# First quarter of the output weights split beside the prompt's attention, the others in pieces, in a GLA + MLA decoder step

## The chip, the cores and the metric

One core of one Trainium2 chip runs the whole step in one launch. The metric is the device time of an execution in microseconds, the median over several runs. TensorE (PE, with its weight loads PEld) makes all matrix products; VectorE (DVE), ScalarE (ACT) and GpSimd (POOL) do the rest; SyncE (SP) issues most transfers, GpSimd the gathers of cache pages. Each engine takes its instructions in the order in which they stand.

## What is computed

One decoder layer for a prompt of 1024 tokens and 8 samples of 8 new tokens with 8192 cached ones each, all in fp32. The layer norms its input, projects it, and mixes tokens by two groups of heads side by side: gated linear attention (GLA, a recurrence in chunks) and latent attention (MLA, softmax over latent rows; the samples' rows come from a paged cache). The two outputs, 512 columns each, are joined, projected by w_o (1024 x 1024), gated and added to the input; a gated convolutional FFN follows.

```
def mla_attend(q_lat, q_rope, kv, kr, q_pos, k_pos):
    ...
        s = jnp.einsum('bthl,bsl->bhts', ql, kv) + jnp.einsum('bthr,bsr->bhts', qr, kr)
        s = s.astype(jnp.float32) * scale
        s = jnp.where(k_pos[None, :] <= qp[:, None], s, -jnp.inf)
        p = jax.nn.softmax(s, axis=-1).astype(kv.dtype)
        return jnp.einsum('bhts,bsl->bthl', p, kv)
```

## The kernel before

An fp32 product is made as three fp32r products of a high and a low part (`mm3`, L141 to L143): hi x hi, lo x hi, hi x lo. The high part is a cast on ScalarE, the low part a subtraction, mostly on VectorE (L122). Weights go through `block` (L1384): a raw tile `uraw` of 1 MB is loaded by SyncE (L1388), cast to `uhi` (L1393), and subtracted to `ulo`. There are two raw tiles, so the load of a third block waits until the first is subtracted.

The stages are: the input projections; the samples' queries; then two generators that `interleave` draws step by step; then the output projection (`out_proj`), the FFN up and the FFN down. The first generator is `mla_sample`, 32 blocks of 1024 cached keys. For each block GpSimd gathers the rows L (1 MB) and R (256 KB); TensorE transposes them (`kps`, L1227, two PSUM buffers) and ScalarE copies them to KT and KR (L1229); then come the scores S (L1237, L1239), the maximum `rm`, its spread `mg` and `nm` on VectorE, the exponential `p` on ScalarE, its transpose `pt` on VectorE (L1266), the output O (L1271), its sum `on` (L1276). The second is `main`: the prompt's queries, GLA (its rows go from `o_sb` to the DRAM tile `s_mix`, L788), and `mla_prompt`. This one goes over 4 heads: `keys` (products `sps` of a head's key weights `ukr`, split into `uks`), `scores`, `vals`, `values` (probabilities transposed to `pt`, L1158, cast to `pth`, subtracted to `ptl`, products `olps`), then a norm per head (`ob`, sums `hms`) and a store of 256 rows to `s_mix` (L1178). Queries come by `qlr` (L1103) and `qrr` (L1107), the causal mask by `craw` (L1058).

`interleave` is given a total for each generator and always draws from the one whose drawn share of its total is lowest; the sample's instructions get a priority that is put off by up to 450 places, less and less toward its end. A tile scheduler then sets the order on each engine from priorities, dependences, its own model of durations, and free tiles. A pool that is opened late gets its place from the pools closed before it. `main` ends with opening the weights' pools and the gate's, and `out_weights`, four quarters of w_o (256 columns each) through `block`.

`out_proj` takes row blocks `mx` of 128 rows back from `s_mix` (L1419), transposes them (`tps`, L1426), splits them to `mh` and `ml`, and multiplies them by the four quarters (`y`).

Of the kernel before, what the change touches and what calls it, by code (L numbers as in the profile page):

```python
# [11 lines left out]
F32 = mybir.dt.float32  # L12
# [9 lines left out]
P = 128  # L22
# [84 lines left out]
class Kernel:  # L107
# [935 lines left out]
                next(chain, None)  # L1043


    def mla_prompt(self):
        nc, A = self.nc, self.A
        with ExitStack() as es:
            kp = es.enter_context(self.pool("mk"))
            bp = es.enter_context(self.pool("mb", bufs=1))  # L1050
# [3 lines left out]
            pq = es.enter_context(self.pool("psq", bufs=1, space=PSUM))  # L1054
            kTh, kTl = self.kTh, self.kTl
            causal = kp.tile([P, P], F32R, name="causal")
            craw = kp.tile([P, P], F32, name="craw")
            nc.sync.dma_start(craw, A["c_causal"])  # L1058
            nc.scalar.copy(causal, craw)
            def split2(x, name):  # L1060

                n = x.shape[2]
                t = bp.tile([P, TP], F32R, name=name, tag="pp", bufs=4)[:, 0:4 * n].rearrange("p (j a n) -> p j a n", j=2, a=2)
                nc.scalar.copy(t[:, 0], x)
                self.lo(t[:, 1], x, t[:, 0], nc.vector)
                return t

            def keys(h):

                raw = bp.tile([P, 2, P], F32, name="ukr", tag="ukr")  # L1070
                nc.sync.dma_start(raw, A["w_mla_uk"][0, :, h].rearrange("(a p) n -> p a n", p=P))
                uk = split2(raw, "uks")
                K = [kp.tile([P, TP], F32R, name=x, tag=x) for x in ("Kh", "Kl")]
                for s0 in (0, 512):
                    so = slice(s0, s0 + 512)
                    ps = psS.tile([P, 512], F32, name="sps", tag="S")
                    for a in range(2):
                        self.mm3(ps, uk[:, 0, a], uk[:, 1, a], kTh[:, a, so], kTl[:, a, so], a == 0, a == 1)
                    nc.scalar.copy(K[0][:, so], ps)
                    self.lo(K[1][:, so], ps, K[0][:, so], nc.vector)  # L1080
                    yield 1.3
                self.K = K

            def vals(pr):

                uv = split2(self.uv[:, :, 256 * pr:256 * pr + 256], "uvs")
                V = [mv.tile([P, 8, 256], F32R, name=x, tag=x) for x in ("vh", "vl")]
                for j0 in range(0, 8, 2):
                    ps = psS.tile([P, 512], F32, name="sps", tag="S").rearrange("p (j n) -> p j n", j=2)
                    for j in range(2):  # L1090
                        o = slice((j0 + j) * P, (j0 + j + 1) * P)
                        for a in range(2):
                            self.mm3(ps[:, j], kTh[:, a, o], kTl[:, a, o], uv[:, 0, a], uv[:, 1, a], j == 0 and a == 0, j == 1 and a == 1)
                    x = slice(j0, j0 + 2)
                    nc.scalar.copy(V[0][:, x], ps)
                    self.lo(V[1][:, x], ps, V[0][:, x], nc.vector)
                    yield 1.3
                self.V = V
# [83 lines left out]
            for h in range(4):  # L1182
                yield from keys(h)
                for m in range(4):
                    yield from scores(h, m)
                    if len(self.pend) > 1:
                        yield from values(*self.pend.pop(0))
                    if m == 0 and h % 2 == 0:
                        yield from vals(h // 2)
            while self.pend:  # L1190
                yield from values(*self.pend.pop(0))


    def mla_sample(self, es):
# [186 lines left out]
        self.new = o1, m1, l1  # L1381


    def block(self, src, eng, wp=None):  # L1384

        shape = [P, src.shape[1], src.shape[2]]
        raw = self.wp[0].tile(shape, F32, name="uraw", tag="uraw", bufs=2)
        self.nc.sync.dma_start(raw, src)  # L1388
        if wp is None:
            hi, lo = self.pair(shape)  # L1390
        else:
            hi, lo = (wp.tile(shape, F32R, name=x, tag=x, bufs=2) for x in ("uhi", "ulo"))
        self.nc.scalar.copy(hi, raw)  # L1393
        self.lo(lo, raw, hi, eng)
        return hi, lo

    def pair(self, shape, k=None):
# [5 lines left out]
    def out_weights(self):  # L1403
        nc, A = self.nc, self.A
        wo = A["w_o"][0].rearrange("(a p) n -> p a n", p=P)
        self.wo = [self.block(wo[:, :, 256 * q:256 * q + 256], nc.vector) for q in range(4)]

    def out_proj(self, es, ds):
        nc, A = self.nc, self.A
# [275 lines left out]
    def run(self, stop=None):  # L1685
        nc = self.nc
        with ExitStack() as es:
            dp = es.enter_context(self.pool("scratch", space=DRAM))
            self.s_kv = dp.tile([T, LAT + 2 * RO], F32, name="s_kv")
            self.s_qn = dp.tile([4, P, TP], F32, name="s_qn")  # L1690
            self.s_qr = dp.tile([2, P, TP], F32, name="s_qr")
            self.s_qk = dp.tile([4, P, T], F32, name="s_qk")
            self.s_la = dp.tile([T, 256], F32, name="s_la")
            self.s_v = dp.tile([T, 512], F32, name="s_v")
            self.s_r = dp.tile([T, 512], F32, name="s_r")
            self.s_mix = dp.tile([T, D], F32, name="s_mix")
            self.s_x2 = dp.tile([T, D], F32, name="s_x2")
            self.s_gate = dp.tile([2, 65, D], F32, name="s_gate")
            self.s_g = dp.tile([NCH, P, T], F32, name="s_g")
            self.s_ml = dp.tile([1, 512], F32, name="s_ml")  # L1700
            self.cp = cp = es.enter_context(self.pool("const"))
            self.constants(cp)
            self.ada_start(cp)
            fs = es.enter_context(ExitStack())
            gs = es.enter_context(ExitStack())
            ds = es.enter_context(ExitStack())
            with ExitStack() as zs, ExitStack() as xs:
                self.zp = zs.enter_context(self.pool("z"))
                self.xp = xs.enter_context(self.pool("x", bufs=2, side="right"))
                self.phase1()  # L1710
                if stop == "z":
                    return
                with ExitStack() as es2:
                    self.sample_queries(zs, xs, ds, es2)
                    if stop == "q":
                        return

                    mk = es2.enter_context(self.pool("mkT", side="right"))

                    def main():  # L1720
                        yield from self.prompt_queries(self.prompt_keys(mk, self.nq, self.pq))
                        zs.close()
                        yield from self.gla()
                        yield from self.mla_prompt()
                        self.wp = [fs.enter_context(self.pool(f"fw{j}")) for j in range(2)]
                        self.gt = gs.enter_context(self.pool("gate"))
                        self.out_weights()
                        yield 0.0

                    self.ep = es2.enter_context(self.pool("me", bufs=1, side="right"))  # L1730
                    self.interleave((self.mla_sample(es2), 429.0, 450), (main(), 244.5, 0))
            if stop == "mix":
                return
            with ExitStack() as hs:
                with self.pool("pt", bufs=2, space=PSUM) as self.pt, self.pool("pu", space=PSUM) as self.pu:
                    hT = self.out_proj(hs, ds)
                    gs.close()
                    if stop == "wo":
                        return
                    self.ffn_up(hT)  # L1740
                    if stop == "up":
                        return
            self.ffn_down()
# [35 lines left out]
```

## Time and profile before

| | us |
|---|---|
| median of 3 runs | 1860.03 |
| lowest, highest | 1857.51, 1861.93 |
| profiled execution, its own time | 1861.26 |
| span in its trace | 1859.5 |
| TensorE busy | 1797.6 |
| VectorE busy | 930.1 |
| ScalarE busy | 708.9 |
| GpSimd busy | 529.8 |

The span is what the trace covers, from the first to the last instruction; the execution's own time has 1.8 us around it. A row of the trace's timeline gives start, duration, engine, line, operation, the tiles written and read, and shapes; in brackets is the idle time of the engine before it and what ended that. PE rows of a few products that follow each other are put into one. SyncE's rows (SPq) show the time that the issuing took, waits within it included.

### The profile page before, as it was taken

What the parts mean: (1) busy time and instruction counts of PE and PEld (TensorE: products, weight loads), DVE (VectorE), ACT (ScalarE), POOL (GpSimd) and SP (SyncE); (2) the same over time, 40 slices, a digit from 0 to 9 for tenths busy, and PEclk for the clock granted to TensorE, in tenths of its full rate; (3) what the DMA queues carried; (4) which work ended last, traced back from release to release, by engine and by line L of the source; (5) the groups of instructions that cost most, each with busy time, mean ns of one, the idle gap of its engine ahead of it and who ended that gap; (6) DMA issues with size and microseconds to landing.
All of it is one profiled execution on the core that took longest, in us unless ns stands there. A gap on an engine that the chain in (4) does not pass through costs nothing.

```text
span 1859.5 us, 30758 instructions
## 1 busy us (share of the span) xinstructions
PE 1797.6 (97%) x12403; PEld 1500.4 (81%) x12403; DVE 930.1 (50%) x1680; ACT 708.9 (38%) x1398; POOL 529.8 (28%) x567
## 2 busy tenths in 40 slices
PE   6999999999999999999799999999999999999998
PEld 3888766765665776777499999999999999788787
DVE  3731233347784555565556755554545554523433
ACT  2461111455666666667523422222222222323322
POOL 2640100423554223323011133333333331202221
PEclk7999999999999999999899999999999999999999
DMA  8255552666655555455542412111222111834463
GB/s 300 87 160 181 181 172 75 248 210 199 212 197 166 203 196 173 161 184 181 181 149 104 137 65 71 65 59 65 72 70 70 65 61 61 266 98 136 146 183 96
DMA packets 170618, 265.26 MB, mean 143 GB/s; under 512 B 18278, under 2 KB 118694, under 8 KB 162283
## 3 DMA queue, kind: packets, MB, share of 16 engines
q1 hardware_dynamic: 156138, 179.39, 29.8%
q0 software_dynamic: 14336, 83.89, 13.0%
q8 instruction: 98, 1.61, 0.4%
q14 instruction: 46, 0.37, 0.1%
HBM read 221.49 MB, written 41.75 MB: 142 GB/s over the span
## 4 chain that ended last, share of the span: by engine, by line
PE 70%; DVE 3%; DMA 2%; ACT 1%; issue 1%; SPq 0%; POOL 0%; DVEq 0%; POOLq 0%; ACTq 0%
PE ups L141 9%; PE ups L143 9%; PE ups L142 9%; PE kps L1227 6%; PE yps L143 4%; PE yps L141 4%; PE yps L142 4%; PE S L1237 3%; PE O L1271 3%; PE y L141 2%; PE y L143 2%; PE y L142 2%; PE S L1239 1%; PE lps L705 1%; PE sps L141 1%; PE sps L142 1%
## 5 line engine op out<-in xcount | busy, mean ns | idle before, releaser
L141 PE MATMUL ups<-gh,uhi 128*128 128x384 f32 (+1 forms) x1056 | 347.2, 329 | 0.3 <-DVE hraw L343 0.3
L142 PE MATMUL ups<-gl,uhi 128*128 128x384 f32 (+1 forms) x1056 | 346.7, 328 | 0.0
L143 PE MATMUL ups<-gh,ulo 128*128 128x384 f32 (+1 forms) x1056 | 346.5, 328 | 0.0
L1565 DVE TENSOR_SCALAR cv<-u,vt 128x1024 f32<-128x1024 f32 (+1 forms) x88 | 133.2, 1535 | 216.3 <-ACT u L1555 179.3
L141 PEld LDWEIGHTS ups<-gh,uhi 128*128 128x128 f32 x1056 | 198.3, 188 | 0.7 <-DVE hraw L343 0.6
L143 PEld LDWEIGHTS ups<-gh,ulo 128*128 128x128 f32 x1056 | 198.3, 188 | 0.1
L142 PEld LDWEIGHTS ups<-gl,uhi 128*128 128x128 f32 x1056 | 198.3, 188 | 0.0
L1229 ACT COPY KT<-kps 128x512 f32<-128x512 f32 x256 | 145.3, 587 | 101.3 <-PE kps L1227 100.3
L122 POOL TENSOR_TENSOR ulo<-uraw,uhi 128x2048 fp32r<-128x2048 f32 x24 | 111.4, 4643 | 207.6 <-ACT uhi L1393 204.7
L1555 ACT COPY u<-ups 128x384 f32<-128x384 f32 (+1 forms) x130 | 57.6, 444 | 278.7 <-PE ups L143 278.7
L1227 PEld LDWEIGHTS kps<-ident,L 128*128 128x128 f32 x1024 | 111.5, 141 | 62.0 <-issue 43.4
L1227 PE MATMUL kps<-ident,L 128*128 128x128 f32 x1024 | 153.3, 280 | 4.1 <-ACT KT L1229 2.5
L143 PE MATMUL yps<-uhi,gl 128*128 128x512 f32 x341 | 133.3, 392 | 5.2 <-DVE gl L122 5.2
L141 PE MATMUL yps<-uhi,gh 128*128 128x512 f32 x341 | 133.2, 391 | 0.0
L142 PE MATMUL yps<-ulo,gh 128*128 128x512 f32 x341 | 133.1, 391 | 0.0
L122 DVE TENSOR_TENSOR gl<-graw,gh 128x1408 fp32r<-128x1408 f32 x31 | 59.1, 1908 | 130.2 <-ACT gh L1612 130.2
L1218 POOL DMA_INDIRECT R<-cache_krope,idx x64 | 66.5, 1039 | 179.3 <-PE kps L1227 141.4
L1612 ACT CAST gh<-graw 128x1408 fp32r<-128x1408 f32 (+1 forms) x35 | 45.7, 1306 | 158.7 <-PE yps L142 130.1
L1393 ACT CAST uhi<-uraw 128x2048 fp32r<-128x2048 f32 (+1 forms) x38 | 70.8, 1862 | 92.5 <-PE ups L142 67.1
L141 PE MATMUL zps<-whi,hh 128*128 128x512 f32 (+2 forms) x256 | 96.0, 375 | 0.0
L143 PE MATMUL zps<-whi,hl 128*128 128x512 f32 (+2 forms) x256 | 94.2, 368 | 0.8 <-DVE hl L122 0.8
L1571 POOL TENSOR_TENSOR gl<-gl,cv 128x1088 f32<-128x1088 f32 x22 | 56.0, 2544 | 135.3 <-ACT gl L1570 135.3
(443 smaller groups left out, 3803.5 us busy)
## 6 DMA issues: line engine op xcount, KB each, us to landing
wraw<-w_ada SPq DMA_DIRECT2D x48, 512.0 KB
uraw<-w_ffn_up SPq DMA_DIRECT2D x22, 1024.0 KB
graw<-s_g SPq DMA_DIRECT2D x32, 704.0 KB
s_g<-gl SPq DMA_DIRECT2D x22, 544.0 KB
uraw<-w_ffn_down SPq DMA_DIRECT2D x10, 1024.0 KB
xt<-x_prompt SPq DMA_DIRECT2D x16, 512.0 KB
wraw<-w_in SPq DMA_DIRECT2D x12, 512.0 KB
uraw<-w_o SPq DMA_DIRECT2D x4, 1024.0 KB
```

Source lines behind the costliest of these rows:

```text
L122: eng.tensor_tensor(out, x, hi.bitcast(F32), ALU.subtract)
L141: mm(out, wh, xh, start=start, stop=False)
L142: mm(out, wh, xl, start=False, stop=False)
L143: mm(out, wl, xh, start=False, stop=stop)
L1218: nc.gpsimd.indirect_dma_start(R.rearrange("p j l -> p (j l)"), None, ck, io)
L1227: nc.tensor.transpose(ps[:, k], x, self.ident)
L1229: nc.scalar.copy(KT[:, q // 2, j0:j0 + 4] if q < 4 else KR[:, 4 * half:4 * half + 4], ps)
L1237: nc.tensor.matmul(S[r], Q[:, c], KT[:, c, :, r], start=(c == 0), stop=False)
L1393: self.nc.scalar.copy(hi, raw)
L1555: copy(u[:, 2 + c0:2 + c0 + m], ps[:, 0:m])
L1565: nc.vector.tensor_scalar(yv[z], sh(2)[z], self.cw2[:, ch:ch + 1], self.cb[:, ch:ch + 1], ALU.mult, ALU.add)
L1571: nc.gpsimd.tensor_tensor(gl, gl, res[0], ALU.mult)
```

## The change

`mla_prompt` gets the weights' generator. The pool `fw0` is opened before it, `fw1` and the gate's behind its heads. After the third head's steps (h == 2) the first quarter of w_o is drawn, the other three at the end. `block` casts and subtracts in four pieces of 512 elements for each partition where it took 2048 at once. The causal mask's raw tile shares the tile `ukr`. The sample's total in `interleave` is 418 for 429, while its steps add up to 428.8 as before: drawn shares of it count higher, so it is drawn later, and its priority is put off less.

```
-    def mla_prompt(self):
+    def mla_prompt(self, weights):
...
-            craw = kp.tile([P, P], F32, name="craw")
+            craw = bp.tile([P, 2, P], F32, name="ukr", tag="ukr")[:, 0]
...
+                if h == 2:
+                    self.wo = [next(weights)]
             while self.pend:
                 yield from values(*self.pend.pop(0))
+        self.wp.append(self.fs.enter_context(self.pool("fw1")))
+        self.gt = self.gs.enter_context(self.pool("gate"))
+        self.wo += weights
...
-    def block(self, src, eng, wp=None):
+    def block(self, src, eng, wp=None, parts=1):
...
-        self.nc.scalar.copy(hi, raw)
-        self.lo(lo, raw, hi, eng)
+        n = shape[1] // parts
+        for j in range(parts):
+            o = slice(j * n, j * n + n)
+            self.nc.scalar.copy(hi[:, o], raw[:, o])
+            self.lo(lo[:, o], raw[:, o], hi[:, o], eng)
...
-        self.wo = [self.block(wo[:, :, 256 * q:256 * q + 256], nc.vector) for q in range(4)]
+        for q in range(4):
+            yield self.block(wo[:, :, 256 * q:256 * q + 256], nc.vector, parts=4)
...
-                        yield from self.mla_prompt()
-                        self.wp = [fs.enter_context(self.pool(f"fw{j}")) for j in range(2)]
-                        self.gt = gs.enter_context(self.pool("gate"))
-                        self.out_weights()
+
+                        self.wp = [fs.enter_context(self.pool("fw0"))]
+                        yield from self.mla_prompt(self.out_weights())
                         yield 0.0
...
-                    self.interleave((self.mla_sample(es2), 429.0, 450), (main(), 244.5, 0))
+                    self.interleave((self.mla_sample(es2), 418.0, 450), (main(), 244.5, 0))
```

Line numbers of the changed kernel are 5 higher in `mla_sample`, 5 to 9 higher in the weights and the projection. What stands on SyncE at the start of the prompt's attention before, from GLA's last stores on (brackets hold the queues and engines that an instruction waits for):

```order
L788 DMA s_mix<-o_sb 128x2x512 [waits DMAHW3_49,Pool_49]
L785 DMA rg<-s_r 128x2x512 [waits DMAHW4_49,DMAHW2_49]
L780 DMA o_gla_p<-S 128x2x128 [waits DMAHW5_49,DVE_49]
L1058 DMA craw<-c_causal 128x128 [waits DMAHW6_49,PE_49]
L788 DMA s_mix<-o_sb 128x2x512 [waits Pool_49]
L1071 DMA ukr<-w_mla_uk 128x2x128 [waits DMAHW0_49,PE_49]
L1103 DMA qlr<-s_qn 128x256 [waits DMAHW1_49]
L1107 DMA qrr<-s_qr 64x256
L1107 DMA qrr<-s_qr 64x256 [waits DMAHW3_49]
L1107 DMA qrr<-s_qr 64x256 [waits DMAHW4_49,PE_49]
```

And in the changed kernel:

```order
L780 DMA o_gla_p<-S 128x2x128 [waits DMAHW3_49,DVE_49]
L788 DMA s_mix<-o_sb 128x2x512 [waits DMAHW4_49,Pool_49]
L1058 DMA ukr<-c_causal 128x128 [waits PE_49]
L1103 DMA qlr<-s_qn 128x256 [waits DMAHW6_49,DMAHW7_49,DMAHW4_49,DMAHW1_49]
L1107 DMA qrr<-s_qr 64x256 x3
L1107 DMA qrr<-s_qr 64x256 [waits DMAHW2_49]
L1393 DMA uraw<-w_o 128x8x256 [waits DMAHW3_49,PE_49,Activation_49]
L1393 DMA uraw<-w_o 128x8x256
L1071 DMA ukr<-w_mla_uk 128x2x128 [waits DMAHW5_49,Activation_49]
```

The store of GLA's last rows now stands ahead of the mask, `qlr` waits for more transfers (that store's among them), and two loads of w_o stand ahead of the first `ukr`. ScalarE at the same place, before:

```order
L1229 COPY KR<-kps 128x512 [waits PE_49]
L1229 COPY KT<-kps 128x512 [waits PE_49,Activation_49]
L1059 CAST causal<-craw 128x128 [waits DMAHW6_49]
L1229 COPY KT<-kps 128x512 [waits PE_49] x3
L1229 COPY KR<-kps 128x512 [waits PE_49,Activation_49]
L1255 ACTIVATE p,rs<-S,nm 128x512 [waits DVE_49]
L1229 COPY KT<-kps 128x512 [waits PE_49] x4
L1229 COPY KR<-kps 128x512 [waits PE_49]
L1229 COPY KT<-kps 128x512 [waits PE_49,Activation_49]
L1064 CAST uks<-ukr 128x256 [waits DMAHW0_49]
L133 CAST qlsh<-qlr 128x256 [waits DMAHW4_49,DMAHW1_49]
```

And now:

```order
L1234 COPY KR<-kps 128x512 [waits PE_49,Activation_49]
L1234 COPY KT<-kps 128x512 [waits PE_49]
L1059 CAST causal<-ukr 128x128 [waits DMAHW6_49,DMAHW5_49]
L133 CAST qlsh<-qlr 128x256 [waits DMAHW4_49,DMAHW2_49,DMAHW6_49,DMAHW0_49,Pool_49]
L1234 COPY KT<-kps 128x512 [waits PE_49] x3
L1401 CAST uhi<-uraw 128x512 [waits DMAHW3_49]
L1401 CAST uhi<-uraw 128x512
L1234 COPY KR<-kps 128x512 [waits PE_49]
L1401 CAST uhi<-uraw 128x512 x2
L1234 COPY KT<-kps 128x512 [waits PE_49,Activation_49]
L1064 CAST uks<-ukr 128x256 [waits DMAHW5_49]
```

The query cast `qlsh` moved up to the mask, and the four casts of the first quarter stand around a copy KR, ahead of `uks`. TensorE at the sample's end, before (S from KR is its last score, `tps` the first work of the output projection):

```order
L143 MATMUL olps<-pth,vl 128x128
L1237 MATMUL S<-KT,Qd 32x512 [waits Activation_49]
L1237 MATMUL S<-KT,Qd 32x512 x3
L1239 MATMUL S<-KR,Qd 32x8x32 [waits Activation_49]
L1239 MATMUL S<-KR,Qd 32x8x32 x7
L1173 MATMUL pt<-ident,ol 128x128 [waits Activation_49]
L1173 MATMUL pt<-ident,ol 128x128
L1271 MATMUL O<-L,pt 32x256 [waits DVE_49]
L1271 MATMUL O<-L,pt 32x256 x15
L1281 MATMUL fps<-small,on 128x32 [waits DVE_49]
...
L1284 MATMUL lps<-ln,small 32x1 [waits Activation_49]
L1426 MATMUL tps<-ident,mx 128x128 [waits DMAHW0_49]
```

And now, from the last score on:

```order
L1244 MATMUL S<-KR,Qd 32x8x32 [waits Activation_49]
L1244 MATMUL S<-KR,Qd 32x8x32 x7
L141 MATMUL olps<-pth,vh 128x256 [waits Activation_49]
...
L143 MATMUL olps<-pth,vl 128x256
L1158 MATMUL pt<-ident,p 128x128 [waits PE_49]
L1158 MATMUL pt<-ident,p 128x128 x2
L141 MATMUL olps<-pth,vh 128x256 [waits Activation_49]
...
L143 MATMUL olps<-pth,vl 128x128
L1276 MATMUL O<-L,pt 32x256 [waits DVE_49]
L1276 MATMUL O<-L,pt 32x256 x15
L1173 MATMUL pt<-ident,ol 128x128 [waits Activation_49]
L1173 MATMUL pt<-ident,ol 128x128
```

Twelve products `olps` and three transposes `pt`, which stood ahead of the last score, now stand between it and the last O. SyncE at the same place, before:

```order
L1178 DMA s_mix<-ob 128x2x128 [waits DMAHW0_49,DVE_49]
L1178 DMA s_mix<-ob 128x2x128 [waits DMAHW1_49,DVE_49]
L1178 DMA s_mix<-ob 128x2x128 [waits DVE_49]
L1388 DMA uraw<-w_o 128x8x256 [waits DMAHW3_49,PE_49]
L1388 DMA uraw<-w_o 128x8x256 [waits DMAHW4_49,PE_49,Activation_49]
L1178 DMA s_mix<-ob 128x2x128 [waits DMAHW5_49,DVE_49]
L1388 DMA uraw<-w_o 128x8x256 [waits DMAHW6_49,DMAHW3_49,DVE_49]
L1388 DMA uraw<-w_o 128x8x256 [waits DMAHW7_49,DMAHW4_49,DVE_49]
L1419 DMA mx<-s_mix 128x1024 [waits DMAHW0_49,PE_49]
L1419 DMA mx<-s_mix 128x1024 [waits DMAHW1_49]
```

And now:

```order
L1178 DMA s_mix<-ob 128x2x128 [waits DMAHW1_49,DVE_49]
L1178 DMA s_mix<-ob 128x2x128 [waits DMAHW2_49,DVE_49]
L1178 DMA s_mix<-ob 128x2x128 [waits DVE_49]
L311 DMA gt_10602<-s_gate 128x1024 [waits DMAHW4_49,PE_49]
L312 DMA gt_10602<-s_gate 64x1024 [waits DMAHW5_49]
L1393 DMA uraw<-w_o 128x8x256 [waits DMAHW6_49,DVE_49]
L1393 DMA uraw<-w_ffn_up 128x8x256 [waits DMAHW7_49,DVE_49]
L1178 DMA s_mix<-ob 128x2x128 [waits DMAHW0_49,DVE_49]
L1428 DMA mx<-s_mix 128x1024 [waits DMAHW1_49]
L1428 DMA mx<-s_mix 128x1024 [waits DMAHW2_49]
```

Three of the four quarters are not issued here any more (the second and third had their raw tiles earlier), the gate's two loads are, and a load of w_ffn_up stands where the last quarter's was, ahead of the last store and of `mx`.

## Rows read from the trace of the kernel before

**Rows 1.** Page: busy time, share of the span and instructions of each engine.
```profile
PE 1797.6 (97%) x12403; PEld 1500.4 (81%) x12403; DVE 930.1 (50%) x1680; ACT 708.9 (38%) x1398; POOL 529.8 (28%) x567
```

**Rows 2.** Stretches: us, busy PE, PEld, DVE, ACT, POOL, PEclk, DMA share, GB/s.
```profile
320.00:589.45 269.45, 257.36 (x2581) 173.54 (x2579) 164.98 (x453) 155.72 (x340) 110.88 (x116) 0.99 0.61 203
589.45:609.40 19.95, 17.99 (x167) 9.98 (x167) 6.12 (x16) 12.12 (x26) 9.57 (x9) 1.00 0.72 255
609.40:909.60 300.20, 297.35 (x2717) 217.78 (x2715) 163.24 (x479) 197.98 (x476) 85.94 (x111) 1.00 0.52 176
909.60:925.90 16.30, 5.38 (x44) 2.67 (x41) 11.22 (x20) 8.33 (x10) 0.93 (x2) 0.67 0.57 200
925.90:935.50 9.60, 8.60 (x38) 8.03 (x39) 7.04 (x7) 3.03 (x6) 0.00 (x0) 0.50 1.05 364
```

**Rows 3.** Groups by line, whole span: busy us, mean ns of one, idle before.
```profile
L1227 PE MATMUL kps<-ident,L 128*128 128x128 f32 x1024 | 153.3, 280 | 4.1 <-ACT KT L1229 2.5 <-DMA L<-cache_latent,idx 1.3
...
L1237 PE MATMUL S<-KT,Qd 128*32 128x512 f32 x512 | 72.2, 604 | 0.7 <-ACT ML L1285 0.7
```

**Rows 4.** Timeline of TensorE at the sample's end: start us, duration us.
```profile
903.77 0.28 PE L141 MATMUL olps<-pth,vh 128*128 128x256 f32 x1
903.88 0.28 PE L142 MATMUL olps<-ptl,vh 128*128 128x256 f32 x1
...
908.57 1.05 PE L1239 MATMUL S<-KR,Qd 128*32 128x256 f32 x16
...
916.70 3.64 PE L1271 MATMUL O<-L,pt 128*32 128x256 f32 x32 [6.71 <-DVE pt L1266]
...
925.87 1.97 PE L1426 MATMUL tps<-ident,mx 128*128 128x128 f32 x8 [2.34 <-DMA mx<-s_mix]
```

**Rows 5.** Timeline of VectorE: a small split, then the sample's end.
```profile
619.54 0.69 DVE L122 TENSOR_TENSOR uvs<-uv,uvs 128x512 fp32r<-128x512 f32 x1 [0.34 <-ACT uvs L1064]
...
896.00 0.69 DVE L1242 TENSOR_REDUCE rm<-S 128x1 f32<-128x512 f32 x1 [1.81 <-PE S L1239]
...
899.00 0.71 DVE L1266 STREAM_TRANSPOSE pt<-p 128x512 f32<-128x512 f32 x1
...
911.33 0.40 DVE L798 TENSOR_REDUCE hms<-hsq 128x2 f32<-128x256 f32 x1
...
913.74 2.29 DVE L122 TENSOR_TENSOR ulo<-uraw,uhi 128x2048 fp32r<-128x2048 f32 x1
```

**Rows 6.** Timeline of ScalarE at the sample's end.
```profile
911.53 1.89 ACT L1393 CAST uhi<-uraw 128x2048 fp32r<-128x2048 f32 x1
...
921.20 1.90 ACT L1393 CAST uhi<-uraw 128x2048 fp32r<-128x2048 f32 x1 [5.13 <-DMA uraw<-w_o]
```

**Rows 7.** Timeline of SyncE's queue at the sample's end.
```profile
913.85 0.37 SPq L1178 DMA_DIRECT2D s_mix<-ob  x1
916.05 3.29 SPq L1388 DMA_DIRECT2D uraw<-w_o  x2
919.44 1.01 SPq L1419 DMA_DIRECT2D mx<-s_mix  x2
```

**Rows 8.** Timeline of SyncE's queue at the start of the prompt's attention.
```profile
575.41 0.36 SPq L788 DMA_DIRECT2D s_mix<-o_sb  x1
...
587.94 0.42 SPq L1058 DMA_DIRECT2D craw<-c_causal  x1
600.31 0.36 SPq L788 DMA_DIRECT2D s_mix<-o_sb  x1
...
602.14 2.54 SPq L1107 DMA_DIRECT2D qrr<-s_qr  x4
```

**Rows 9.** Timeline of ScalarE at the end of GLA.
```profile
582.81 0.59 ACT L768 COPY o_sb<-ops 128x512 f32<-128x512 f32 x1 [1.72 <-DMA s_mix<-o_sb]
...
596.03 0.30 ACT L1059 CAST causal<-craw 128x128 fp32r<-128x128 f32 x1 [0.45 <-DMA craw<-c_causal]
```

More of the change, by code (lines that the diff above doesn't have):

```diff
@@ L1703, in run @@
             self.ada_start(cp)
-            fs = es.enter_context(ExitStack())
-            gs = es.enter_context(ExitStack())
+            self.fs = fs = es.enter_context(ExitStack())
+            self.gs = gs = es.enter_context(ExitStack())
             ds = es.enter_context(ExitStack())
```

## Prediction

> **What bounds the kernel now.** I read the page's table of busy time first, then a table of stretches, then the single instructions of the two stretches that the change touches. TensorE is busy 97% of the span; no other engine gets past half of it [rows 1]. So what counts is work added to or taken from TensorE (there is none here: the same products are made) and the microseconds in which it stands idle. The stretches [rows 2] show where those are. GLA (320.00 to 589.45) leaves 12.1 of 269.45 us idle; the way from GLA's last product to the first key product of the prompt's attention (589.45 to 609.40) 2.0 of 19.95; the prompt's attention (to 909.60) 2.9 of 300.2; the way from the sample's last score to the first transposed rows of the output projection (909.60 to 925.90) 10.9 of 16.3. In the 9.6 us behind that the granted clock is 0.50, the 1.2 GHz level, after this idle time; before it, it was 1.00. The change is built for the last gap, and it pays for it in the second stretch.
>
> What fills the tail gap is read from four views. The last score product ends at 908.57 + 1.05 = 909.62 [rows 4]; I call that z. TensorE then waits 6.71 us for the sample's transposed probabilities, and later 2.34 us for the first row block `mx` [rows 4]. On SyncE's queue `mx` stands behind four loads of w_o, of which the last two wait until a split of an earlier quarter has given its raw tile back [rows 7]; ScalarE's casts and VectorE's subtractions of those quarters are 1.9 and 2.3 us each [rows 5, 6]. The transposes start at 925.87 = z + 16.25.
>
> **The tail, step by step.** (1) The order puts 12 value products and three transposes, which stood ahead of the sample's last score, behind it. A value product takes 0.12 us (start to start, 903.77 to 903.88) [rows 4], so with the transposes some 1.8 us of TensorE work moves over and the last score ends at z' = z - 1.8. (2) From there the softmax goes as in the block before: from the maximum's start to the transposed probabilities 899.00 + 0.71 - 896.00 = 3.7 us [rows 5]; the maximum starts some 0.3 later behind a subtraction, so the last O starts at z' + 4. The products behind z' keep TensorE busy for half of that. (3) VectorE then has quarter 1 in four pieces with the sample's and the prompt's last outputs between them, then quarter 2. A 2048-element subtraction is 2.29 us, a 512-element one 0.69 [rows 5]; in pieces a quarter costs 4 x 0.69 = 2.8, 0.5 more. Counted along the new order, quarter 1 is done at z' + 7.7, quarter 2 at z' + 10.6. (4) The last store to s_mix comes 913.85 - 911.33 = 2.5 us behind VectorE's sum `hms` [rows 5, 7], so at z' + 13.2. It now stands on SyncE's queue behind a load of w_ffn_up that waits for quarter 2's split; before, the load that waited there waited for the split of quarter 1, so `mx` is behind two splits still. Taking quarter 0 out takes less than one split's time from this chain. (5) `mx` is issued at z' + 13.6. In the trace it was issued at 919.44 and there at 925.87, 6.4 us, beside 2 MB of w_o [rows 4, 7]. A load of 1 MB took 921.20 - 916.05 = 5.15 us [rows 6, 7]. After the change 1 MB of w_ffn_up is half through when `mx` starts; I take 3.8 (bounds 2.6, half of 5.15, and 6.4). So the transposes start at z' + 17.4 = z + 15.6: **gain 0.65 us**, between a loss of 2.0 and a gain of 1.9; with the 1.0 us that TensorE is idle in the 9.60 us behind it [rows 2], a gain of 3 at most. TensorE still has some 11 us idle there, so I leave the 0.50 clock as it is.
>
> The gate's rows (768 KB) are also loaded in this stretch now, ahead of the last quarter; the order has them waiting for the last value products, at about z', and 7 us lie until the quarter can be loaded. Nothing.
>
> **The start of the prompt's attention.** The order puts the first quarter's load and split here, not beside head 3: the scheduler moves them up to where their tile is free. On SyncE: the last store of GLA's output, causal mask, the first query rows `qlr` with a wait on that store's completion (not there before: other tiles lie there now), four `qrr`, two pieces of weights, the first key weights `ukr`. ScalarE gets the cast `qlsh` of these rows and half of the quarter's casts ahead of a copy KR of sample keys; TensorE's transposes have two PSUM buffers, so it stops two copies later.
> Times from 589.45: the store is issued at 600.31, 10.9 [rows 8]. Its duration: the store before took from 575.41 until ScalarE could write its tile again at 582.81, 7.4 us [rows 8, 9], and at the least the 5 us of a 1 MB load [rows 6, 7]. Then 0.4 for `qlr`, 2.2 for the `qrr` (2.54 with the last's end) [rows 8], 5.15 for w_o, and two casts of a quarter of 1.89 us with the copy behind, 1.6: KR is written at 25.3 to 27.7. TensorE comes there as follows. The new totals (418 for 429) draw the sample later: 24 transposes and 8 scores fewer stand in GLA and as many more ahead of the first key product, 24 x 153.3/1024 + 8 x 72.2/512 = 4.7 us [rows 3]. So TensorE has 18.0 + 4.7 = 22.7 us of work there and needs KR from 20.5 on. The stall is 2.8 to 7.2 us, and the 2.0 us of gaps that this stretch had go into it: **loss 0.8 to 5.2, taken 2.5**, under the middle, since the DMA engines are at 0.72 in this stretch, not full [rows 2]. If that store and w_o share the DMA engines badly with the gathers, it is up to 8: the causal mask, 64 KB, was issued at 587.94 and was used at 596.03, 8.1 us later [rows 8, 9]. And it may be nothing or a gain of 1 to 2, if the added sample work covers all.
> The Trainium skill (DMA: Bandwidth & Descriptors, section "Queues, rings and completion order") says that each DMA engine goes round between the queues that have work for it, a packet at a time; so a load in SyncE's queue would get only its share beside the gathers, which is a queue of its own. The 8.1 us of the mask [rows 8, 9] agree; by that rule the stall would be at its upper end, which is rival A.
>
> **GLA and the rest.** GLA loses 4.7 us of cover; its idle share is 12.1/269, so some 0.2 us more, at most 3: **0.3**. Beside the prompt's attention the sample catches up; it stands 16 to 20 transposes further ahead by head 3, which empties no place: 0. The pieces' 0.5 us on VectorE lie under TensorE there (163 of 300 us busy [rows 2]): 0; if that cover were gone, 0.5.
> The Trainium skill (VectorE: DVE Perf Modes, section "The TRN2 errata — SBUF-src ops pay a fixed extra latency per instruction") says that each instruction pays a fixed time whatever its size, which speaks against pieces. The trace agrees: 0.69 for 512 elements, 2.29 for 2048 [rows 5]. By it three quarters in the tail would cost 1.4 us more on VectorE; by the order only some 1.0 of it is ahead of `mx`, and the sum has that.
>
> **Sum.** -0.65 + 2.5 + 0.3 = +2.1 us. The profiled execution took 1861.26, so 1863.4; in terms of the median 1860.03, which is what is compared, **1862.1**. A measurement of this kernel tells about 0.2% (3.7 us) from no change; this is less.
>
> **Rivals.** *A, slower: the first quarter's casts hold TensorE at the start.* SyncE waits for the whole store, the w_o loads go beside gathers, ScalarE is in order and KR stands behind the casts. Loss 5.2 to 8, with the tail's 0.65 and GLA's 0.3 +4.9 to +7.7: 1865 to 1868. It decides over 0.2% when store and load together take over some 12 us. For it: the 7.4 and 8.1 us. Against: the same 0.72 of the DMA engines [rows 2].
> *B, faster: the tail gives what it was built for and the start is covered.* The store takes 5 us or less, the 4.7 us of added sample work hide the rest and the 2.0 us of gaps there too; in the tail `mx` comes at its lower bound, a gain of up to 3. Together -3.7 to -5: 1855 to 1856.5. For it: 10.9 us idle are there to be had. Against: the order keeps two splits ahead of `mx`.
> *C: it does not do what it says.* The quarter is gone from the tail, but the gate's rows and w_ffn_up's load take its place: tail 0, start +0.8: about 1861.
>
> **Chances.** Forecast (with its own range, 1860 to 1863.7) 0.32, A 0.32, B 0.24, C 0.12. Part of the forecast's upper end is over the bound and some of B under it: faster 0.24, same 0.42, slower 0.34. The range reaches over most of A and B: 1855 to 1867.5.
>
> **What would show it.** In the profile after: TensorE's waits between GLA's last product and the first key product (for ScalarE's KT or KR: 3 to 7 us right, under 1 says B); ScalarE's waits there on w_o or `qlr`; the time from the last score to the first transposed rows (17.4, with the last score 1.8 us earlier); `mx` as the wait that ends last; the clock at 0.50 behind it. I am wrong if the start shows no wait, if the last O waits for VectorE's pieces, or if GLA's idle time grows by more than 3 us.

## The result, and the profile after

The changed kernel takes 1872.76 us in the median (1870.65 to 1876.72), the kernel before 1859.94 on the same chip: ratio 1.0071, interval 1.0059 to 1.0082. It is 12.8 us slower, and outside the range that was forecast. The stretches of the profile after, cut at the same events as in [rows 2] (projection's end, last GLA product, first key product, last score, first transposed rows, first product of the FFN up; columns as there):

```profile
320.31:581.94 261.63, 250.87 (x2509) 168.61 (x2511) 163.64 (x440) 151.32 (x330) 104.16 (x113) 0.99 0.61 204
581.94:618.65 36.71, 23.93 (x239) 13.51 (x239) 12.72 (x35) 17.92 (x40) 12.47 (x12) 0.94 0.77 261
618.65:923.54 304.89, 300.59 (x2700) 218.87 (x2700) 159.47 (x476) 197.38 (x474) 85.88 (x111) 0.99 0.49 164
923.54:941.61 18.07, 5.87 (x55) 3.73 (x55) 12.91 (x31) 8.79 (x21) 0.93 (x2) 0.73 0.66 223
941.61:1059.49 117.88, 117.88 (x977) 116.69 (x978) 73.85 (x103) 39.45 (x68) 15.69 (x34) 0.98 0.35 123
```

The same five of the kernel before took 268.7, 19.9, 300.25, 16.25 and 121.1 us. GLA got shorter by 7.1 (5.8 of the sample's work, 1.3 of idle time); the stretch behind it grew by 16.8, of which 6.0 is that work and 10.8 idle time; the attention grew by 4.6; the tail by 1.8; what follows the tail shrank by 3.2. The sum is +13.0; the two profiled executions, 1872.21 and 1861.26, differ by 10.9, so what lies outside these stretches took some 2 us less. The loss is at the start of the prompt's attention. What TensorE waited for there, from a table of its waits from 581 to 640 (total, times, longest):

```profile
PE sps L141 <- ACT uks L1064: 7.2, 1, 7.2
PE kps L1232 <- ACT KT L1234: 2.7, 5, 1.1
PE S L1244 <- ACT KR L1234: 1.6, 1, 1.6
```

ScalarE's cast `uks` of the first key weights comes last, and the timelines of ScalarE and then SyncE say why:

```profile
602.90 0.40 ACT L133 CAST qlsh<-qlr 128x256 fp32r<-128x256 f32 x1 [2.58 <-DMA qlr<-s_qn]
...
607.55 1.14 ACT L1401 CAST uhi<-uraw 128x512 fp32r<-128x512 f32 x2 [2.43 <-DMA uraw<-w_o]
608.60 0.58 ACT L1234 COPY KR<-kps 128x512 f32<-128x512 f32 x1
...
618.19 0.41 ACT L1064 CAST uks<-ukr 128x256 fp32r<-128x256 f32 x1 [7.49 <-DMA ukr<-w_mla_uk]
```

```profile
593.07 0.36 SPq L788 DMA_DIRECT2D s_mix<-o_sb  x1
593.48 0.46 SPq L1058 DMA_DIRECT2D ukr<-c_causal  x1
598.83 0.33 SPq L1103 DMA_DIRECT2D qlr<-s_qn  x1
599.21 2.38 SPq L1107 DMA_DIRECT2D qrr<-s_qr  x4
601.69 1.15 SPq L1393 DMA_DIRECT2D uraw<-w_o  x2
602.94 1.91 SPq L1071 DMA_DIRECT2D ukr<-w_mla_uk  x1
```

128 KB of key weights, issued by 604.85, are there 13.3 us later. Ahead of them in SyncE's queue stand 2 MB of w_o, and GpSimd's gathers run beside. In 4 us steps (a table of stretches, columns as above) the DMA engines are full until the key weights are there, and TensorE's clock falls to its lower level, 1.2 GHz, in the wait:

```profile
606.00:610.00 4.00, 2.44 (x29) 0.99 (x28) 1.57 (x3) 2.45 (x5) 1.90 (x2) 1.00 1.14 369
610.00:614.00 4.00, 1.41 (x16) 0.84 (x8) 1.62 (x3) 0.70 (x2) 0.00 (x0) 1.00 1.01 403
614.00:618.00 4.00, 0.00 (x0) 0.00 (x0) 0.00 (x0) 0.00 (x0) 0.00 (x0) 0.55 1.03 328
618.00:622.00 4.00, 3.35 (x10) 2.77 (x11) 1.62 (x10) 1.77 (x4) 0.00 (x0) 0.50 0.58 183
622.00:626.00 4.00, 4.00 (x23) 3.01 (x26) 1.96 (x4) 2.71 (x8) 0.40 (x1) 0.67 0.00 0
```

So the wait is paid a second time in part: the 6.35 us from 618.65 to 625 ran at 0.53, about 3 us of lost work (an estimate: 0.47 of 6.35).

### The profile page after: what moved, and what is told of

It is laid out like the page before. It is cut to its first block, busy times and chain, and to the rows that moved or that the text cites. A ratio compares the mean times of both kernels' runs of the same rounds, so it can differ in the third digit from the quotient of the medians.

```text
span 1870.4 us, 30758 instructions
## 1 busy us (share of the span) xinstructions
PE 1798.5 (96%) x12403; PEld 1499.0 (80%) x12403; DVE 931.2 (50%) x1692; ACT 709.3 (38%) x1410; POOL 525.9 (28%) x567
## 3 DMA queue, kind: packets, MB, share of 16 engines
q0 software_dynamic: 14336, 83.89, 12.9%
## 4 chain that ended last, share of the span: by engine, by line
PE 83%; DVE 6%; DMA 5%; ACT 2%; POOL 1%; issue 1%; SPq 1%; POOLq 0%; DVEq 0%; ACTq 0%
PE ups L141 9%; PE ups L143 9%; PE ups L142 9%; PE kps L1232 6%; PE yps L143 4%; PE yps L142 4%; PE yps L141 4%; PE zps L141 3%; PE zps L143 3%; PE zps L142 3%; PE S L1242 3%; PE O L1276 3%; PE y L141 2%; PE y L142 2%; PE y L143 2%; PE adaps L249 2%
## 5 line engine op out<-in xcount | busy, mean ns | idle before, releaser
L1401 ACT CAST uhi<-uraw 128x2048 fp32r<-128x2048 f32 (+2 forms) x50 | 71.9, 1461 | 92.3 <-PE ups L142 67.2
```

What stands on the lines that cost most here:

```text
L1401: self.nc.scalar.copy(hi[:, o], raw[:, o])
```

## Experiments

Theory 1 was that this load and its place in the queue are the cause; theory 2 was rival A of the prediction (the casts on ScalarE, and the wait for the store); theory 3 that the new total misplaces the sample's work. A table of all kernels stands at the end of this section. A ratio is taken from several executions beside the kernel before on the same chip; where one time stands in its place, it is a single execution, and then the profile carries the reading (the executions of one kernel lie up to some 12 us apart here).

**The quarter's load held back.** A tiny VectorE copy into the raw tile makes the load wait for the third head's sums, and the second quarter's for the first's split.

```
+        if after is not None:
+            self.nc.vector.tensor_copy(raw[0:1, 0, 0:1], after)
         self.nc.sync.dma_start(raw, src)
...
+                    self.after = self.pend[-1][3][0:1, 0:1]
                     self.wo = [next(weights)]
+                    self.after = self.wo[0][1][0:1, 0, 0:1].bitcast(F32)
```

> The changed kernel with one tiny VectorE copy more for each of the first two quarters of w_o: their raw tiles take one number from the third head's sums (quarter 0) or from quarter 0's split (quarter 1) before they are loaded, so that the loads can't be issued at the start of the prompt's attention. Theory 1 (the first key weights' load stands behind 2 MB of w_o on full DMA engines, TensorE waits 7.2 us for it, and then runs at the 1.2 GHz level for 6 us): the wait and the low clock go, 11 to 14 us, so 1859 to 1862. Theory 2 (the quarter's casts on ScalarE ahead of a copy of sample keys, and the queries' wait for GLA's last store, hold TensorE): the casts go, the store's wait stays, so 1862 to 1866. Theory 3 (the new totals leave GLA and the start with the wrong share of the sample): nothing changes, 1870 or more.

Ratio 1.0074 (1.0047 to 1.0101), 1876.90 beside 1862.87: no gain, against theory 1 as I had put it; of the three forecasts only theory 3's (1870 or more) fits the time. But the wait at the start is gone (idle 4.4 us in that stretch, from 12.8). The same key weights, with no w_o ahead of them, were there 2.35 us after their issue (601.49 to 603.84; SyncE, then ScalarE):

```profile
600.97 0.52 SPq L1071 DMA_DIRECT2D ukr<-w_mla_uk  x1
```

```profile
603.84 0.40 ACT L1064 CAST uks<-ukr 128x256 fp32r<-128x256 f32 x1 [0.68 <-DMA ukr<-w_mla_uk]
```

And the attention has 10.0 idle where it had 4.3. TensorE's longest wait in it, and ScalarE at the same place:

```profile
821.73 1.91 PE L1244 MATMUL S<-KT,Qd 128*32 128x512 f32 x8 [4.75 <-ACT KT L1236]
```

```profile
819.02 2.18 ACT L1405 CAST uhi<-uraw 128x512 fp32r<-128x512 f32 x4 [3.47 <-DMA uraw<-w_o]
821.10 0.57 ACT L1236 COPY KT<-kps 128x512 f32<-128x512 f32 x1
```

The load was issued at 809.33 and the casts stand on ScalarE 6 us later, with the copies of the sample's keys behind them: the load is late, and the products run at the lower clock again (1.91 us where 1.06 is usual). The order had moved a wait of this kind 200 us on. This gave theory 4: wherever casts of w_o stand on ScalarE sooner than their load is there, TensorE stops two copies later.

**The mask's tile in its own place.**

```
-            craw = bp.tile([P, 2, P], F32, name="ukr", tag="ukr")[:, 0]
+            craw = kp.tile([P, P], F32, name="craw")
```

> The changed kernel with the causal mask's raw tile in a place of its own again, as in the kernel before: in the order the first key weights' load then stands ahead of the two loads of w_o; those loads and the first quarter's casts stay at the start. Theory 1: TensorE's wait for the key weights' cast falls from 7.2 to under 2 us and the low clock with it, so 1862 to 1866. Theory 2: the casts still hold the copy KR, so over 1868. Theory 3: 1870 or more.

Ratio 1.005 (1.0026 to 1.0075), 1870.21 in the median: the wait falls as theory 1 gave it (under 2 us), the time does not (1862 to 1866). The first key weights are now issued at 596.38, ahead of w_o, and TensorE's wait for `uks` is 0.86 us, though they stand right behind GLA's last store of 512 KB and took 8.4 us from 597.19 on. But the casts still wait, and hold the copies behind the first key product: the attention has 8.35 idle, with these two waits in it:

```profile
615.14 1.31 PE L1244 MATMUL S<-KR,Qd 128*32 128x256 f32 x16 [2.39 <-ACT KR L1234]
...
623.10 0.66 PE L1232 MATMUL kps<-ident,L 128*128 128x128 f32 x4 [1.97 <-ACT KT L1234]
```

The first is theory 4 again: a cast of w_o had waited 3.15 us for its load. Ahead of the second stands ScalarE's cast of the next query rows, which waited 1.23 us for a load issued behind w_o:

```profile
621.31 0.40 ACT L133 CAST qlsh<-qlr 128x256 fp32r<-128x256 f32 x1 [1.23 <-DMA qlr<-s_qn]
```

**One quarter ahead of the key weights in place of two.** Only the second quarter's load is held.

```
+                    self.after = None
                     self.wo = [next(weights)]
+                    self.after = self.wo[0][1][0:1, 0, 0:1].bitcast(F32)
```

> The changed kernel with only the second quarter's load held until the first is split: 1 MB instead of 2 stands ahead of the first key weights' load, whose place in the queue is the same. Theory 1: the key weights land some 3 to 5 us earlier, TensorE waits 2 to 4 us for their cast where it waited 7.2, so 1866 to 1869. Theory 2 and 3: no change, 1871 to 1873.

1868.03 us in one execution, beside 1862.87 before. The stretch behind GLA is 29.5 us for 36.7, its idle time 6.0 for 12.8. The key weights were there 7.9 us after their issue at most (603.71 to 611.56), with the DMA engines just as full (1.03 from 604 to 612), and TensorE did not wait for `uks` at all, where theory 1 had 2 to 4 us. The low clock is shorter but not gone:

```profile
612.00:616.00 4.00, 4.00 (x18) 3.46 (x17) 2.60 (x12) 1.69 (x4) 0.00 (x0) 0.60 1.00 385
```

So halving what stands ahead of the key weights takes the 7 us off: theory 1 in its place, and in size by this one time.

**Casts held, loads left at the start.** The opposite of the previous ones: the first quarter's high part takes a number from the third head's sums before it is cast.

```
+        if then is not None:
+            self.nc.vector.tensor_copy(hi[0:1, :, 0:1], then.rearrange("p (a n) -> p a n", n=1).broadcast_to([1, shape[1], 1]))
```

> The changed kernel with the first quarter's casts on ScalarE held until the third head's scores, while the two loads of w_o stay at the start, ahead of the first key weights' load. Theory 1 (the key weights' load behind them): TensorE still waits 5 us or more there for the key weights' cast, 1866 to 1871. Theory 2 (the casts on ScalarE): that wait falls under 2 us, 1862 to 1865.

1876.80 us in one execution, beside 1865.11 before, above what either theory gave (1866 to 1871, 1862 to 1865). With no cast of w_o on ScalarE there, TensorE waits even longer for the key weights (table of TensorE's waits from 560 to 640: total, times, longest):

```profile
PE sps L141 <- ACT uks L1064: 8.9, 1, 8.9
```

So at the start it is the loads, not the casts: theory 2 falls for the wait on `uks` of the kernel as it was changed (the 1.6 us for KR there are gone without the casts). The third load of w_o, which the changed kernel issues at 611.05, is not issued here before 650, so the wait does not need it. In the last 2 us before its cast (621 to 623) the mean share of the DMA engines is only 0.07 to 0.08; what the load still waits for then is open.

**Load and casts far apart.** The first quarter's load is held until the second head's scores, its casts until the third head's (both copies above, with the first's source taken after the second head).

> The changed kernel with the first quarter's load held until the second head's scores are done and its casts on ScalarE until the third head's are, by tiny VectorE copies; the second quarter's load is held until the first is split. So the load has some 70 us of its own before the casts stand on ScalarE. Theory 4 (ScalarE takes its work in order, so a cast of w_o whose load is not there yet holds the copies of sample keys behind it and so TensorE, wherever it stands; in the run with the late load that was 4.75 us at 821.73): TensorE's idle time in the attention falls from 10 to under 4.5 us and its start stays as in that run, so 1862 to 1866. Theory 3 (the rest of the change costs it): still 1868 or more.

Ratio 1.0028 (1.0017 to 1.0039). The start has 4.5 idle and the attention 4.6, as theory 4 has it; the median, 1867.22, is a little above what it gave (1862 to 1866). So with both waits gone 0.43 of the 0.71% is gone too; the 0.28% that is left is not in these waits.

**The rest of the change by its parts.** First the total alone on the kernel before:

```
-                    self.interleave((self.mla_sample(es2), 429.0, 450), (main(), 244.5, 0))
+                    self.interleave((self.mla_sample(es2), 418.0, 450), (main(), 244.5, 0))
```

> The kernel before with the sample's total 418 for 429 and nothing else. Theory 1: small, 1859 to 1862, with GLA's end some 7 us earlier and the stretch behind it as much longer. Theory 3: over 1866, with more idle time in GLA or behind it.

Ratio 1.0001 (0.9984 to 1.0017): by itself the total costs nothing, and theory 3 falls as the whole cause. GLA is 7.1 us shorter, as in the changed kernel, and the attention 9.9 longer. The changed kernel with 429 again:

> The changed kernel with the sample's total 429 again. The start's order on SyncE is the same, so by theory 1 the stall there stays; GLA has its 4.7 us of sample work back and the start that much less, which the stall then does not cover: 1872 to 1877. By theory 3 the time falls by 5 or more, under 1867.

Ratio 1.0045 (1.0026 to 1.0063). The stall at the start stayed (idle 9.0), as theory 1 had it, but the time fell by 0.26% (the intervals just touch), to 1870.59, against theory 1 (1872 to 1877) and short of theory 3 (under 1867). GLA did not get its sample work back (261.9 us, as with 418), so my reason for a loss was wrong: the early quarter shifts the sample's work in the order by itself, and the total does too. The stall is 4 us smaller because the key weights, behind the same 2 MB, were there after 9.2 us (605.28 to 614.53) and not 13.3; why is open. Its profile is also of its fastest execution, 1865.58. So 13.3 us is no fixed price: with 2 MB ahead the four kernels that have them there show 9.2 to 13.7. The kernel before with total and pieces, so without the early quarter:

> The kernel before with the total 418 and the four pieces, so the change without the early first quarter, its pools and the shared mask tile. If the early quarter is what costs, this is within 3 us of the kernel before, 1858 to 1863; if pieces or totals cost, 1866 or more.

Ratio 1.0003 (0.999 to 1.0016): all the loss hangs on the early quarter and what came with it (its pools, the mask's shared tile). The changed kernel without pieces:

> The changed kernel with casts and subtractions of w_o in one piece again. If pieces cost what their fixed time says, 0.5 us on VectorE for a quarter, two quarters stand ahead of the first row block in the tail, so 1 us less, 1871 to 1872; if pieces let the sample's last steps through between them, 1 to 3 us more. The start is as in the changed kernel.

Ratio 1.0072 (1.005 to 1.0094), so no difference from the changed kernel's 1.0071 that could be told. And the pieces alone, `parts=4` in the kernel before, 429:

> The kernel before with the four pieces and nothing else of the change (total 429). In the run with pieces and the total 418 the tail and the way to the FFN's first product took 3.7 us less than in the kernel before, and the attention up to there 2.8 us more, as with the total 418 alone. If both hold by themselves, this is 3 to 4 us faster than the kernel before, ratio 0.998; if the gain hung on the total, no change.

Ratio **0.9975** (0.9959 to 0.9992), 1859.49 beside 1865.11: its interval lies under the kernel before. With the total 418 the same pieces gained nothing that could be told (1.0003 beside 1.0001), so the gain stands on one comparison of two. A place where pieces save time is the first 3.2 us steps behind the first transposed rows (columns as above; before, then the kernel before with pieces and 418, then with the pieces alone):

```profile
925.87:929.07 3.20, 2.64 (x10) 2.07 (x10) 2.50 (x2) 1.89 (x4) 0.00 (x0) 0.50 1.01 366
929.07:932.27 3.20, 2.76 (x13) 2.76 (x14) 3.20 (x5) 0.59 (x1) 0.00 (x0) 0.50 1.05 383
932.27:935.47 3.20, 3.20 (x17) 3.20 (x16) 1.34 (x3) 0.59 (x1) 0.00 (x0) 0.50 1.09 350
```

```profile
926.88:930.08 3.20, 3.05 (x12) 2.48 (x13) 3.20 (x6) 2.33 (x5) 0.00 (x0) 0.50 1.00 352
930.08:933.28 3.20, 3.20 (x27) 3.20 (x26) 3.01 (x5) 1.17 (x2) 0.00 (x0) 0.92 1.02 382
933.28:936.48 3.20, 3.20 (x29) 3.20 (x28) 0.67 (x1) 0.00 (x0) 0.00 (x0) 1.00 1.09 354
```

```profile
931.38:934.58 3.20, 3.20 (x13) 2.70 (x14) 3.09 (x6) 2.11 (x4) 0.00 (x0) 0.50 1.00 357
934.58:937.78 3.20, 3.20 (x18) 3.20 (x17) 2.97 (x4) 0.59 (x1) 0.00 (x0) 0.53 1.07 390
937.78:940.98 3.20, 3.20 (x29) 3.20 (x28) 0.69 (x1) 0.59 (x1) 0.00 (x0) 1.00 1.07 343
```

In the kernel before TensorE paused there for `ml`, which stands on VectorE behind the last quarter's subtraction:

```profile
929.51 1.11 PE L1426 MATMUL tps<-ident,mx 128*128 128x128 f32 x4 [1.00 <-DVE ml L122]
```

With pieces `ml` still stands behind all four, but the first subtraction starts behind the first small cast, so the quarter's cast and subtraction take 3.15 us and not 4.22 (ScalarE and VectorE before, then with pieces and 418):

```profile
924.64 1.90 ACT L1393 CAST uhi<-uraw 128x2048 fp32r<-128x2048 f32 x1 [1.42 <-DMA uraw<-w_o]
...
926.57 2.29 DVE L122 TENSOR_TENSOR ulo<-uraw,uhi 128x2048 fp32r<-128x2048 f32 x1 [1.14 <-ACT uhi L1393]
```

```profile
925.86 2.18 ACT L1396 CAST uhi<-uraw 128x512 fp32r<-128x512 f32 x4
...
926.51 2.50 DVE L122 TENSOR_TENSOR ulo<-uraw,uhi 128x512 fp32r<-128x512 f32 x4 [0.63 <-ACT uhi L1396]
```

The pause is 0.15 us with pieces and 418, and none with the pieces alone. The granted clock was 0.50 for 9.6 us before; with 418 it was 0.92 in the second step, with the pieces alone, without any pause, only in the third 1.00. So the pause does not by itself settle when the clock comes back. The way to the FFN's first product took 121.1 us before, 121.0 with the total alone, 117.9 with total and pieces, 118.9 with pieces. The pieces' profile is of an execution of 1866.19, 6.7 above its median, so it shows a place of the gain and not the whole of it.

**The early quarter in its best place.** Mask's tile apart, load after the second head, casts after the third, total 429, pieces:

> The early first quarter in the best place that I can give it: the mask's tile in a place of its own, the quarter's load held until the second head's scores, its casts until the third head's, the total 429, pieces. By theory 4 the start's and the attention's waits are as in the kernel before, and what is left is the early quarter itself in the tail: its idle time was 2 us longer there than without it. So 0 to 2 us slower than the kernel with the pieces alone, 1857 to 1861. If an early quarter costs by some other way, 1863 or more.

Ratio 1.0016 (1.0002 to 1.0031), 1868.9 in the median, so about 0.4% over the pieces alone: not the 1857 to 1861 that I gave it, but over 1863, the branch in which the early quarter costs by some other way. Its attention has 4.6 idle, its start 3.9; and its tail is 17.5 us for 16.0 with the pieces alone. There the order puts two quarters' subtractions ahead of the last output's sums: from the last score's end the last store goes out after 926.63 - 917.96 = 8.7 us, with the pieces alone after 920.73 - 915.42 = 5.3. What else the 0.4% consists of is not settled; single profiles of a stretch differ by some us here (GLA took 274.0 in the one of the pieces alone, 268.7 in the one before, with the same work).

Idle time of TensorE by stretch in each kernel (stretch less busy time, us, from one profile each), with the ratio to the kernel before or the one time:

| kernel | start | attention | tail | behind | result |
|---|---|---|---|---|---|
| before | 2.0 | 2.9 | 10.9 | 1.0 | 1 |
| changed | 12.8 | 4.3 | 12.2 | 0.0 | 1.0071 |
| load held to the third head | 4.4 | 10.0 | 13.8 | 0.0 | 1.0074 |
| mask's tile apart | 3.8 | 8.4 | 12.8 | 0.0 | 1.005 |
| one quarter ahead | 6.0 | 4.3 | 11.7 | 0.0 | 1868.03 (before 1862.87) |
| casts held | 13.8 | 3.1 | 13.4 | 0.0 | 1876.80 (before 1865.11) |
| load and casts apart | 4.5 | 4.6 | 13.1 | 0.0 | 1.0028 |
| total 429 | 9.0 | 4.0 | 10.8 | 0.0 | 1.0045 |
| whole quarters | 13.6 | 4.3 | 12.4 | 0.0 | 1.0072 |
| before, total 418 | 2.9 | 4.7 | 10.8 | 1.0 | 1.0001 |
| before, 418, pieces | 3.0 | 4.7 | 10.3 | 0.2 | 1.0003 |
| before, pieces | 2.0 | 3.9 | 10.6 | 0.0 | 0.9975 |
| early quarter, best place | 3.9 | 4.6 | 12.2 | 0.0 | 1.0016 |

## Why the prediction was wrong

**The start: the step that failed.** The prediction followed the new chain store, `qlr`, `qrr`, w_o, casts, copy KR, and that chain came as it said: the store took some 5.8 us (593.07 to 598.83; 5 to 7.4), KR was written at 609.18 - 581.94 = 27.2 (25.3 to 27.7), and without the wait for `uks` the stretch's idle time would be 5.5 us, 1.6 of it for KR. (From KR at 25.3 to 27.7 and a need from 20.5 on, the stall is 4.8 to 7.2 and the loss 2.8 to 5.2; the prediction wrote 2.8 and 0.8 for the lower ends, so that the middle of its range was 3.0 and not 4.0.) It stopped there. The order that it quoted has `ukr<-w_mla_uk` behind the two loads of w_o and `uks` as the next cast; the landing of that load was given no price. It is 13.3 us, and the term of 2.5 us (0.8 to 5.2), with GLA's 0.3, was 9.7 (298.3 for 288.7 from the projection's end to the first key product), and some 3 more for the clock behind it, which the prediction had considered in the tail only. A row to ask it from was at hand: in the kernel before the same 128 KB were issued at 600.76 and cast at 608.17, with no w_o ahead and no wait for them.

**Rival A** had the side, the place and the queue beside the gathers right, and the wrong load: its casts on ScalarE were not what held TensorE (the run with the casts held), but for the 1.6 us for KR. Its price of 5.2 to 8 had the causal mask's 8.1 us behind it, a load with only a 128 KB store just ahead in its queue. The rule of the Trainium skill (DMA: Bandwidth & Descriptors, section "Queues, rings and completion order") that each DMA engine goes round between its queues spoke for this side, and the trace does not speak against it: with both at work the DMA engines were at 1.01 to 1.14. But the larger part hung on what stood first in the load's own queue: with one of the 2 MB held and the DMA engines as full, 7 us were gone.

**The tail** came nearly as worked out. The last O started at z' + 4.0 (4), the last store went out at z' + 12.9 (13.2), `mx` at z' + 13.3 (13.6), the transposes at z' + 18.1 (17.4: the load of `mx` took 4.8 us and not 3.8). The rows (TensorE, then SyncE):

```profile
927.56 1.93 PE L1276 MATMUL O<-L,pt 128*32 128x256 f32 x32 [0.17 <-DVE pt L1271]
...
941.61 1.97 PE L1435 MATMUL tps<-ident,mx 128*128 128x128 f32 x8 [9.24 <-DMA mx<-s_mix]
```

```profile
931.27 0.37 SPq L1393 DMA_DIRECT2D uraw<-w_o  x1
934.00 0.37 SPq L1393 DMA_DIRECT2D uraw<-w_ffn_up  x1
936.42 0.37 SPq L1178 DMA_DIRECT2D s_mix<-ob  x1
936.84 0.99 SPq L1428 DMA_DIRECT2D mx<-s_mix  x2
```

The wait for the sample's probabilities in [rows 4] is gone and the wait for `mx` is as much longer: the idle time only changed its name. By the prediction's own count, with 1.8 us of products moved behind the score, the gain up to the transposes was nothing where it had 0.65. "I leave the 0.50 clock as it is" was wrong: the granted clock was 0.89 in the second 3.2 us behind them, where before it stayed at 0.50, and with the pause of 1.0 us gone that gave 3.2 us. So the stretches of the tail changed by -1.4 us in all (+1.8 and -3.2), near the forecast by luck. The pieces in the kernel before have a like gain without the early quarter (0.3 + 2.2 us, with the total 418 0.6 + 3.2), and the early quarter with whole quarters has most of the second part too (118.8 for 121.1).

**GLA** kept its idle time (10.8 for 12.1) when 5.8 us of sample work left it, not 4.7: the loss of 0.3 was none. **The pieces' price** was taken as a cost that hides. The Trainium skill (VectorE: DVE Perf Modes, section "The TRN2 errata — SBUF-src ops pay a fixed extra latency per instruction") says that small instructions pay a fixed time each, and four took 2.49 us in a row where one took 2.29 [rows 5], so the price was 0.2 us and not 0.5. What the prediction left out is that ScalarE's casts and VectorE's subtractions of one quarter then run side by side, 3.15 us for 4.22 in all.

## What to carry over

A transfer that is brought forward has to be followed past its own reader: look at each load that now stands behind it in the same queue, and at who waits for that one, down to the bound engine. Moving the split later helps only if load and cast are far apart, since an engine that takes its work in order stops everything behind a cast whose data is late. And before work is moved out of a gap, ask whether cutting it into pieces there, so that two engines work on it side by side, does as much.

## What the runs showed of the hardware

A wait of 7.2 us of TensorE cost about 3 us more behind it, at a granted clock of 0.50 to 0.53. One load of 128 KB was there 2.35 us after its issue with no w_o ahead in its queue, within 7.9 with 1 MB of w_o, and after 9.2 to 13.7 with 2 MB. Behind the tail's idle time the granted clock was 0.50 for 9.6 us in the kernel before, with a pause of 1.0 us in it; in the kernels with unbroken work there it was 0.89 in the second 3.2 us step (changed) or 0.53 (pieces alone), and 1.00 in the third. Four 512-element subtractions in a row took 2.49 us, less than four times the 0.69 of one.
